# A second product accumulated in PSUM on a ScalarE copy of the first

## The chip, the cores and the metric

The kernel runs on one core of one Trainium2 chip. The metric is the device time of one execution in microseconds (us). The engines are called PE (TensorE), DVE (VectorE), ACT (ScalarE), POOL (GpSimd) and SP (SyncE); POOL and SP issue the transfers here. PSUM, the memory that PE writes, has eight banks of 128 x 512 float32.

## What is computed

One layer of a hybrid decoder on 512 tokens of 1024 channels, in float32, with 256 memory tokens beside them:

```python
h = rmsnorm(x);  proj = h @ w_in
y_a = (B * conv3(C * v)) @ w_a_out                 # short gated convolution
y_b = silu(layernorm(conv31(u * sigmoid(ug)) + bias)) @ w_b_out
y_c = attention(q, rmsnorm(mem) @ w_kv) @ w_att_out
x = x + (g0 * y_a + g1 * y_b + g2 * y_c) @ w_o     # g = sigmoid(gates of h)
gt, up = split(conv3(rmsnorm(x) @ w_up))
x = x + (silu(gt) * up) @ w_down;  return rmsnorm(x)
```

## The kernel before

**Precision.** Each operand of a product is split into a rounded high part and the rest. ACT makes the high part (`whi`, by a job `wh`, L621), DVE subtracts to get the low part (`wlo`, job `wl`, L625). Three matmuls (high x high, high x low, low x high) replace one.

**Quads.** The projections `w_in` and `w_up` are computed in 29 quads: 4 of `glu`, 4 of `cv`, 2 of `q`, 2 of `bb`, 6 of `gate` (the mixer) and 11 of `up` (the feed-forward part). A quad takes two column blocks of 256 and both halves of the tokens and of the 1024 inputs. In place of eight block products it makes seven, by a scheme of Strassen's kind: products of sums of weight blocks with sums of activation blocks, numbered 1, 2, 5, 6, 7, 4, 3. A product is 24 matmuls of 256 columns (`multiply`, L801).

The seven products go to three banks of PSUM. Bank `a` takes 1, then 6, 7 and 4 on top of it; bank `b` takes 5, then 3; bank `c` takes 2 alone. After a product the partial sum is read out (`quad_reads`, L820 to L853) into two SBUF tiles, `first` and `second`:

- `r1` (ACT, L828) copies bank `a` after product 1 to the first half of `first`.
- `r2` (DVE, L836) adds bank `c`, which holds product 2, to that half.
- `r5` and `r4` (ACT, L832, L851) copy to the halves of `second` with a minus; `r6` (ACT, L844) copies bank `a` after product 6 to the second half of `first`; `r7` and `r3` (DVE, L836) subtract and add.

Product 6 waits for `r1`, 7 for `r6`, 4 for `r7`, 3 for `r5`, since they write to the bank that was read. Neighbouring quads overlap on PE: the order is 6, 5 of the next quad, 7, 1 of the next, 4, 2 of the next, 3.

**The rest.** Before the quads stand keys and values from the memory tokens; between them the attention; a convolution of 31 taps in the mixer shared by ACT (products, `tp`, L1369) and DVE (sums, L1376); merge products (L1548 to L1550); the product with `w_o` (L572 to L574) in a seven-product scheme of its own; RMSNorm and transposes; the up quads with their three-tap convolution (L1498, L1504), `silu` and the gated tile `z` (L1867); and the product with `w_down` (L572 to L574, operands `zh` and `zl`, L2054 and L2061).

**Weights.** SP loads blocks of 512 KB (`ld`, L651), and POOL adds other blocks on top of them in flight by accumulating DMAs (L759), so that sums of weight blocks cost no engine time. A POOL DMA waits until the block's earlier use has been split.

**Order.** Each piece of work is a job with an engine, a cost and the jobs it waits for (`Jobs`, L226). PE's sequence is written out by hand (`seq`). A planner (`run`, L324) issues the others in the order of planned start, with ties by a due time: the latest start that PE's sequence allows, shifted by an entry of the table `LATER` for each kind of job (L73); `AHEAD` (L154) bounds for some kinds how early they may come. Buffers are rings of places (`take`), among them `ps`, the eight banks. The order so found on each engine is fixed in the program.

Of the kernel before, what the change touches and what calls it, by code (L numbers as in the profile page):

```python
# [67 lines left out]
UNIT_BUFS = 4  # L68
SUMS_BY_VECTOR = [("glu", 0)]
# [4 lines left out]
    "ACT c3": 3.05, "ACT cf": 151.64, "ACT csq": -59.81, "ACT exp": -90.93, "ACT fh h b00": 71.92,  # L74
    "ACT fh h b10": 0.49, "ACT fh h b11": -0.54, "ACT fh h t5": 18.75, "ACT fh h t6": -5.1,
    "ACT fh h2 t4": -0.3, "ACT fh h2 t5": -104.69, "ACT fh h2 t6": -37.81, "ACT fh h2 t7": -75.17,
    "ACT high": -1310.89, "ACT kh": -15.95, "ACT m root": -362.05, "ACT mgh a": -219.21,
    "ACT mgh b": -0.99, "ACT mgh c": 21.87, "ACT mgh d": -153.36, "ACT mgh e": 33.21,
    "ACT mgh f": -62.81, "ACT mgh g": -271.76, "ACT mh": 3.42, "ACT msq": 232.67,
    "ACT mu high": 145.56, "ACT oh": -157.89, "ACT pth": -125.46, "ACT qh": -99.6,  # L80
# [7 lines left out]
    "ACT sg": -62.24, "ACT sigmoid": -52.69, "ACT silu": 7.01, "ACT sq": -24.79, "ACT sr": -61.22,  # L88
    "ACT swish": -187.08, "ACT tap 0": 386.19, "ACT tap 1": -305.81, "ACT tap 3": -118.04,
# [9 lines left out]
    "ACT xroot": -139.83, "ACT xsq": -336.93, "ACT xsquare": -212.34, "ACT zh a": -65.22,  # L99
    "ACT zh b": -2.97, "ACT zh c": -129.55, "ACT zh d": -36.36, "ACT zh f": 1.48,  # L100
    "ACT zh g": -16.33, "DVE CV": -940.31, "DVE c3": -2.4, "DVE centre": 2.27, "DVE cf": -142.45,
# [5 lines left out]
    "DVE hd": -408.91, "DVE kl": -59.89, "DVE kt": 2.68, "DVE low": -1070.51,  # L107
    "DVE m scale": 21.29, "DVE mgl a": -99.36, "DVE mgl b": -1.83, "DVE mgl c": 45.17,
    "DVE mgl e": 12.48, "DVE mgl f": 89.83, "DVE mgl g": -183.96, "DVE ml": -76.45,
    "DVE ms c": 2.23, "DVE ms d": -43.26, "DVE ms e": -77.92, "DVE ms f": -596.02,  # L110
    "DVE msum": 32.2, "DVE mu fold": 229.47, "DVE mu low": 174.53, "DVE mu sum": 0.09,
    "DVE ol": -67, "DVE pn": -423.21, "DVE ptl": -21.53, "DVE ql": -21.16, "DVE r2 bb": -162.25,
# [6 lines left out]
    "DVE rl": -49.63, "DVE s6 glu": 1.12, "DVE sum": -306.61, "DVE sv": 1.24, "DVE tap 2": -81.17,  # L119
    "DVE tap 3": -12.91, "DVE top": -207.51, "DVE tot1": 70.89, "DVE tot2": -61.79,  # L120
    "DVE um": 13.54, "DVE v scale": -106.89, "DVE var fold": -2.02, "DVE var sum": 76.06,
# [8 lines left out]
    "DVE wsum": 473.99, "DVE x scale": -1037.6, "DVE x1 a": -18.75, "DVE x1 b": 243.92,  # L130
    "DVE x1 c": -180.74, "DVE x1 d": -17.54, "DVE x1 e": -112.02, "DVE x1 f": 46.27,
    "DVE x1 g": 20.12, "DVE xn": 3.93, "DVE xnorm": -39.32, "DVE xsum": -37.83,
    "DVE ymul": -36.44, "DVE ys": -4.73, "DVE z": -64.04, "DVE zd": -330.65, "DVE zl a": -650.04,
    "DVE zl b": -204.45, "DVE zl c": -3.74, "DVE zl d": -392.26, "DVE zl e": -2.42,
    "DVE zl f": -3.2, "DVE zl g": 10.21, "DVE zs d": -29.57, "DVE zs e": 108.61,
    "NONE c3": -206.17, "NONE cf": -314.68, "NONE mem tile": -186.16, "NONE raw tile K": -214.01,
    "NONE raw tile V": -229.8, "NONE rows": -24.01, "NONE sums": 290.26, "NONE temps": 154.52,
# [6 lines left out]
    "POOL wadd x": 0.53, "POOL wadd y": -89.15, "POOL wl merge 0": -554.82,  # L144
# [7 lines left out]
}  # L152

AHEAD = {  # L154
# [2214 lines left out]
```

## Time and profile before

| | us |
|---|---|
| median of 3 runs | 898.55 |
| lowest and highest | 898.41, 900.51 |
| the profiled execution | 899.25 |
| its span in the profile | 897.5 |

The span is what lies between the first and the last instruction of the profile; the other 1.75 us of that execution lie around it. The granted clock of PE was 0.999 of full speed. In the profile's groups, a line such as "L801 PE MATMUL bank<-ft6h,whi" names the line of the code, the engine, the operation and the tiles written and read, then the count, the busy time and the mean of one. In the chain of waits and the timeline the first number is the start, the second the duration.

### The profile page before, as it was taken

To read this page: it belongs to the slowest core of one execution; us is meant where nothing else is said; L and a number is where in the kernel's file an instruction comes from. 1 tells how busy PE (TensorE), PEld (TensorE's weight loads), DVE (VectorE), ACT (ScalarE), POOL (GpSimd) and SP (SyncE) were. 2 spreads that over 40 slices of the span, in tenths; PEclk is the share of its full clock that TensorE was granted. 3 is DMA by queue.
4 is the path that set the end of the run, shared out by engine and by line. 5 is a ranking of instruction groups with operands and counts; after the bars stand their busy time and mean duration, and the time that the engine had idled before them with its cause. 6 is when DMAs were issued, how large, how long until landed. Compare 5 with 4: busy or idle time off the path is not lost.

```text
span 897.5 us, 16787 instructions
## 1 busy us (share of the span) xinstructions
PE 888.1 (99%) x6677; PEld 849.2 (95%) x6677; DVE 835.6 (93%) x953; ACT 666.2 (74%) x911; POOL 126.7 (14%) x153
## 2 busy tenths in 40 slices
PE   8999999999999999999999999999999999999997
PEld 8999999999989999999899988899999999998886
DVE  6897999999999999999997888998899889999998
ACT  7677988989997888767856933777676676766566
POOL 0011121111011211111100001021221121002310
PEclk9999999999999999999999999999999999999999
DMA  9979698866688887988966498399999986769982
GB/s 356 379 184 261 137 224 193 214 157 116 164 203 242 198 177 168 211 218 208 230 127 183 141 338 206 102 234 286 307 241 250 221 174 125 197 243 333 257 196 94
DMA packets 54366, 190.60 MB, mean 212 GB/s; under 512 B 6160, under 2 KB 6544, under 8 KB 54288
## 3 DMA queue, kind: packets, MB, share of 16 engines
q0 software_dynamic: 20880, 75.24, 46.3%
q1 hardware_dynamic: 33120, 114.02, 35.2%
q8 instruction: 52, 0.85, 0.4%
q10 hardware_dynamic: 288, 0.27, 0.1%
q14 instruction: 26, 0.21, 0.1%
HBM read 185.31 MB, written 4.19 MB: 211 GB/s over the span
## 4 chain that ended last, share of the span: by engine, by line
PE 90%; DMA 5%; issue 2%; ACT 1%; DVE 1%; POOL 0%; SPq 0%; DVEq 0%; POOLq 0%; ACTq 0%
PE bank L801 56%; PE bank L572 6%; PE bank L574 6%; PE bank L573 6%; PE bank L1548 5%; PE bank L1550 5%; PE bank L1549 5%; PE bank L1059 2%; DMA wo<-in_w_o 2%; DMA ('up', 3)_946_7137<-in_w_up 1%; DMA wf<-in_w_up 1%; DMA mem<-in_mem_t 1%; PE ss L930 0%; ACT whi L621 0%; DVE wlo L625 0%
## 5 line engine op out<-in xcount | busy, mean ns | idle before, releaser
L621 ACT CAST whi<-wf 128x1024 fp32r<-128x1024 f32 x204 | 211.7, 1044 | 75.7 <-PE bank L801 30.7
L625 DVE TENSOR_TENSOR wlo<-wf,whi 128x1024 fp32r<-128x1024 f32 x198 | 239.1, 1215 | 16.2 <-ACT whi L621 16.1
L1369 ACT ACTIVATE tp<-u,pk 128x507 f32<-128x507 f32 (+22 forms) x184 | 119.8, 708 | 6.6 <-DVE acc L1376 5.3
L1376 DVE TENSOR_TENSOR acc<-acc,tp 128x1022 f32<-128x1022 f32 (+21 forms) x92 | 109.3, 1192 | 1.7 <-ACT tp L1369 0.4
L759 POOL DMA_DIRECT2D wf<-in_w_in x54 | 47.4, 903 | 234.6 <-DVE wlo L625 159.2
L801 PE MATMUL bank<-ft6h,whi 128*128 128x256 f32 x232 | 63.9, 275 | 0.2 <-ACT gt L828 0.2
L801 PE MATMUL bank<-ft5h,wlo 128*128 128x256 f32 x232 | 63.9, 275 | 0.2 <-DVE wlo L625 0.2
L801 PE MATMUL bank<-fb10h,whi 128*128 128x256 f32 x232 | 64.0, 276 | 0.0
L801 PE MATMUL bank<-fb11h,whi 128*128 128x256 f32 x232 | 64.0, 276 | 0.0
L801 PE MATMUL bank<-ft5l,whi 128*128 128x256 f32 x232 | 63.9, 275 | 0.0
L801 PE MATMUL bank<-fb00h,whi 128*128 128x256 f32 x232 | 63.9, 275 | 0.0
L801 PE MATMUL bank<-ft6h,wlo 128*128 128x256 f32 x232 | 63.8, 275 | 0.0
L801 PE MATMUL bank<-fb00l,whi 128*128 128x256 f32 x232 | 63.8, 275 | 0.0
L801 PE MATMUL bank<-fb00h,wlo 128*128 128x256 f32 x232 | 63.8, 275 | 0.0
L801 PE MATMUL bank<-fb10l,whi 128*128 128x256 f32 x232 | 63.8, 275 | 0.0
L801 PE MATMUL bank<-fb10h,wlo 128*128 128x256 f32 x232 | 63.8, 275 | 0.0
L801 PE MATMUL bank<-ft6l,whi 128*128 128x256 f32 x232 | 63.8, 275 | 0.0
L801 PE MATMUL bank<-ft7l,whi 128*128 128x256 f32 x232 | 63.8, 275 | 0.0
L801 PE MATMUL bank<-ft7h,wlo 128*128 128x256 f32 x232 | 63.8, 275 | 0.0
L801 PE MATMUL bank<-fb11l,whi 128*128 128x256 f32 x232 | 63.8, 275 | 0.0
L801 PE MATMUL bank<-fb11h,wlo 128*128 128x256 f32 x232 | 63.8, 275 | 0.0
L801 PE MATMUL bank<-ft7h,whi 128*128 128x256 f32 x232 | 63.8, 275 | 0.0
(378 smaller groups left out, 3134.8 us busy)
## 6 DMA issues: line engine op xcount, KB each, us to landing
wf<-in_w_in SPq DMA_DIRECT2D x58, 512.0 KB, 5.0
wf<-in_w_in POOLq DMA_DIRECT2D x54, 512.0 KB, 6.7
wf<-in_w_up SPq DMA_DIRECT2D x29, 512.0 KB, 8.3
wf<-in_w_up POOLq DMA_DIRECT2D x28, 512.0 KB, 7.5
wf<-in_w_down SPq DMA_DIRECT2D x15, 512.0 KB, 4.7
wf<-in_w_att_out SPq DMA_DIRECT2D x8, 512.0 KB, 3.6
wf<-in_w_a_out SPq DMA_DIRECT2D x8, 512.0 KB, 4.2
wf<-in_w_b_out SPq DMA_DIRECT2D x8, 512.0 KB, 4.6
```

The costliest lines, as they stand in the source:

```text
L572: nc.tensor.matmul(ps, s_hi, w_hi, start=start, stop=False, skip_group_check=again)
L573: nc.tensor.matmul(ps, s_hi, w_lo, start=False, stop=False, skip_group_check=again)
L574: nc.tensor.matmul(ps, s_lo, w_hi, start=False, stop=stop, skip_group_check=again)
L621: nc.scalar.copy(parts[0], src())
L625: nc.vector.tensor_tensor(lo, src(), hi.bitcast(F32), op=ALU.subtract)
L759: nc.gpsimd.dma_start(out=tiles[key], in_=block(w, col[c], k), accum_op=ALU.add)
L801: nc.tensor.matmul(ps[:, c, :], w[:, k, at], in_turns(a[k]), start=first and n == 0, stop=i == 3 and n == 2, skip_group_check=again,)
L1369: nc.scalar.activation(two(("tp", p, s))[:, j, s:], two(("u", p))[:, j, : SEQ - s], AF.Copy, scale=weight(j),)
L1376: nc.vector.tensor_tensor(a, a, two(("tp", p, s))[:, :, s:], op=ALU.add)
L1548: nc.tensor.matmul(ps, w_hi[:, i, at], hi, start=first, stop=False)
L1549: nc.tensor.matmul(ps, w_hi[:, i, at], lo, start=False, stop=False)
L1550: nc.tensor.matmul(ps, w_lo[:, i, at], hi, start=False, stop=last)
```

## The change

A list `SEEDED` names 25 of the 29 quads: all but `glu` 0 and `up` 0 to 2. In these, `r1` no longer reads bank `a` into SBUF: ACT copies it to bank `c` (`seed`). Product 2 does not start bank `c` anew, but accumulates on the copy, and waits for it. `r2` becomes a copy by ACT from bank `c` to the first half of `first`; DVE's addition is gone. `r6` comes after `r2`. Bank `c` is taken by `r1` instead of by product 2, and only a bank that has been written whole before may be taken for it. The quads' numbers of products, matmuls and transfers stay. The tables `LATER` and `AHEAD` are replaced as a whole (314 entries became 305, 183 became 189), and so the order on ACT, DVE, POOL and SP changes through much of the kernel; PE's does not.

```diff
+SEEDED = (
+    [("glu", p) for p in range(1, 4)] + [("cv", p) for p in range(4)]
+    + [(s, i) for s in ("q", "bb") for i in range(2)]
+    + [("gate", br, i) for br in range(3) for i in range(2)] + [("up", q) for q in range(3, 11)]
+)
...
     def multiply(q, f, act):
-        if f in (1, 2, 5):
+        if f in (1, 5) or f == 2 and not seeded(q):
             make(("bank", q, BANK_OF[f]))
...
-                first = f in (1, 2, 5) and i == 0 and c == 0
-                again = not (f in (1, 2, 5) and c == 0)
+                starts = f in (1, 5) or f == 2 and not seeded(q)
+                first = starts and i == 0 and c == 0
+                again = not (starts and c == 0)
...
+        new = f in (1, 5) or f == 2 and not seeded(q)
+        if f == 2 and not new:
+            after.append(("r1", q))
...
+        def seed():
+            make(bank("c"))
+            nc.scalar.copy(tiles[bank("c")], tiles[bank("a")])
+
+        def read2():
+            make(first)
+            nc.scalar.copy(parted(f()[:, :, lo_t]), turned(view("c")))
...
-        job(("r1", q), "ACT", actv(512), read1, [(q, 1)] + list(after),
-            take=[(first, ring)], use=[bank("a")])
-        job(("r2", q), "DVE", dve(512), lambda: add(f()[:, :, lo_t], view("c")),
-            [(q, 2), ("r1", q)], use=[bank("c"), first])
+        if seeded(q):
+            job(("r1", q), "ACT", actv(512), seed, [(q, 1)],
+                take=[(bank("c"), "ps=whole")], use=[bank("a")])
+            job(("r2", q), "ACT", actv(512), read2, [(q, 2)] + list(after), take=[(first, ring)],
+                use=[bank("c")])
+        else:
...
-            [(q, 6), ("r1", q)], use=[bank("a"), first])
+            [(q, 6), ("r2" if seeded(q) else "r1", q)], use=[bank("a"), first])
```

More of the change, by code (lines that the diff above doesn't have):

```diff
@@ L130 @@
[L130 to L135, printed above, removed]
@@ L136 @@
-    "NONE c3": -206.17, "NONE cf": -314.68, "NONE mem tile": -186.16, "NONE raw tile K": -214.01,
-    "NONE raw tile V": -229.8, "NONE rows": -24.01, "NONE sums": 290.26, "NONE temps": 154.52,
[6 rows of a table removed]
-    "POOL wadd x": 0.53, "POOL wadd y": -89.15, "POOL wl merge 0": -554.82,
[7 rows of a table removed]
+    "ACT c3": -120.1, "ACT cf": -509.48, "ACT csq": -53.11, "ACT exp": -0.12,
[3 rows of a table added]
+    "ACT high": -129.98, "ACT kh": 44.12, "ACT m root": -65.33, "ACT mgh a": 248.53,
+    "ACT mgh c": -45.79, "ACT mgh d": -1.43, "ACT mgh e": -192.03, "ACT mgh f": 103.98,
@@ new lines @@
+    "ACT zh d": -45.26, "ACT zh e": -187.1, "ACT zh f": 0.48, "ACT zh g": 68.1, "DVE CV": -69.32,
+    "DVE c3": -40.82, "DVE centre": 122.92, "DVE cf": -0.49, "DVE csum": 200.17,
[4 rows of a table added]
+    "DVE h2 t7": -15.33, "DVE hd": 32.93, "DVE kl": -10.05, "DVE kt": 5.38, "DVE low": -7.04,
+    "DVE m scale": -20.41, "DVE mgl a": -153.33, "DVE mgl b": 81.29, "DVE mgl c": -1,
+    "DVE mgl d": -391.03, "DVE mgl e": -106.25, "DVE mgl f": -46.38, "DVE mgl g": -1.35,
+    "DVE ml": -0.46, "DVE ms c": -5.01, "DVE ms d": 100.31, "DVE ms e": 16.38, "DVE ms f": 12.55,
@@ L152 @@
+    "DVE zs e": -0.21, "NONE cf": -18.86, "NONE mem tile": -38.05, "NONE raw tile V": 2.42,
+    "NONE rows": -0.56, "NONE sums": -330.92, "NONE temps": 8.24, "POOL ea": -45.14,
[5 rows of a table added]
+    "POOL s7 gate": 2.29, "POOL s7 glu": 77.65, "POOL s7 up": 14.62, "POOL wadd e": 41.57,
+    "POOL wadd x": -254.48, "POOL wadd y": 2.91, "POOL wl merge 0": 0.18,
[7 rows of a table added]
 }
 AHEAD = {
-    "ACT exp": 3.5, "ACT fh h b10": 3.6, "ACT fh h b11": 39.1, "ACT fh h t6": 101,
-    "ACT fh h t7": 3.8, "ACT fh h2 t6": 5, "ACT fh h2 t7": 5.3, "ACT high": 1.2, "ACT m root": 51,
@@ L179 @@
-    "DVE sv": 46.7, "DVE top": 52, "DVE tot2": 2.2, "DVE var fold": 1.2, "DVE weigh": 2.6,
[7 rows of a table removed]
-    "NONE c3": 37.8, "NONE cf": 145.6, "NONE raw tile K": 18.2, "NONE raw tile V": 49.2,
-    "NONE rows": 111.3, "POOL s3 glu": 1.2, "POOL s5 glu": 13, "POOL s5 q": 3.9,
[6 rows of a table removed]
+    "ACT cf": 1.6, "ACT csq": 21, "ACT exp": 3.2, "ACT fh h b00": 3.2, "ACT fh h b11": 118,
+    "ACT fh h t4": 1.9, "ACT fh h t6": 48.2, "ACT fh h t7": 7.3, "ACT fh h2 t6": 135.2,
+    "ACT fh h2 t7": 113.1, "ACT high": 61, "ACT m root": 1.3, "ACT mgh b": 19.4,
@@ new lines @@
+    "ACT mgh c": 26.6, "ACT mgh d": 1.1, "ACT mgh e": 10.6, "ACT mh": 16.4, "ACT msq": 1.3,
+    "ACT mu high": 39.9, "ACT pth": 13.7, "ACT qh": 4.2, "ACT r1 bb": 7.8, "ACT r1 cv": 58.5,
[3 rows of a table added]
+    "ACT r5 glu": 58.2, "ACT r5 q": 2.4, "ACT r6 bb": 78.9, "ACT r6 gate": 4, "ACT r6 glu": 31.6,
+    "ACT rh": 1.4, "ACT rm": 57, "ACT sa": 85.7, "ACT sr": 24.9, "ACT tap 2": 17.1,
[4 rows of a table added]
+    "ACT wh0 V": 80.4, "ACT xroot": 4.8, "ACT xsq": 73.9, "ACT zh a": 1.4, "ACT zh c": 101.7,
[3 rows of a table added]
+    "DVE h2 t7": 41.6, "DVE hd": 123.7, "DVE kl": 1.5, "DVE lns": 92.3, "DVE mgl e": 15.9,
@@ new lines @@
+    "DVE mgl f": 3.9, "DVE ml": 2, "DVE ms c": 21.9, "DVE ms f": 23.2, "DVE msum": 4.9,
+    "DVE mu fold": 1.7, "DVE mu low": 1.3, "DVE ol": 8.2, "DVE ptl": 150.2, "DVE ql": 1,
[3 rows of a table added]
+    "DVE var fold": 9.9, "DVE vl": 8.1, "DVE weigh": 6.3, "DVE wl V 0": 39.9,
[4 rows of a table added]
+    "DVE x1 g": 3.2, "DVE xnorm": 16.7, "DVE xsum": 2.8, "DVE ys": 15.9, "DVE z": 1.5,
+    "DVE zl c": 5.6, "DVE zl d": 2.8, "DVE zl e": 86.4, "DVE zl f": 76.9, "DVE zl g": 88.4,
+    "DVE zs d": 100.8, "DVE zs e": 3.6, "NONE c3": 147.6, "NONE cf": 1.5, "NONE raw tile K": 5.3,
@@ L195 @@
+    "NONE raw tile V": 16.1, "NONE rows": 1.1, "NONE sums": 2.6, "NONE temps": 2.6,
[3 rows of a table added]
+    "POOL wadd x": 58, "POOL wadd y": 19, "POOL wl merge 2": 10.7, "POOL xa": 15.7,
[4 rows of a table added]
 }
@@ L301, in latest_starts, with partly @@
         return due, users
+    def partly(self, name):
+        return name[0] in ("ss", "rows") or name[1] in ("warm", "end")
     def free_places(self, ring, leave=0):
+        ring, _, whole = ring.partition("=")
         own, _, other = ring.partition("+")
         own, other = (
-            [(at, r, i) for r in rs.split() for i, at in self.rings[r].items()]
+            [(at, r, i) for r in rs.split() for i, at in self.rings[r].items()
+             if not whole or i in self.written]
             for rs in (own, other)
@@ L393, in run @@
                 self.place[name] = ring, i
+                if ring == "ps":
+                    (self.written.discard if self.partly(name) else self.written.add)(i)
             code = self.tc.nc.cur_bb.bb.instructions
@@ L812, in multiply_job @@
             after.append(("fl", act, OPERAND[f]))
+        new = f in (1, 5) or f == 2 and not seeded(q)
+        if f == 2 and not new:
+            after.append(("r1", q))
         after += {6: [("r1", q)], 7: [("r6", q)], 4: [("r7", q)], 3: [("r5", q)]}.get(f, [])
         pe((q, f), 24 * MM_QUAD, lambda: multiply(q, f, act), after,
-           take=[(bank, "ps")] if f in (1, 2, 5) else [], use=[] if f in (1, 2, 5) else [bank],
-           unit=unit)
+           take=[(bank, "ps")] if new else [], use=[] if new else [bank], unit=unit)
     form_ready = {}
@@ L836, in add @@
             nc.vector.tensor_tensor(parted(t), parted(t), turned(b), op=op)
-        job(("r1", q), "ACT", actv(512), read1, [(q, 1)] + list(after),
-            take=[(first, ring)], use=[bank("a")])
-        job(("r2", q), "DVE", dve(512), lambda: add(f()[:, :, lo_t], view("c")),
-            [(q, 2), ("r1", q)], use=[bank("c"), first])
+        if seeded(q):
[4 more added lines that the diff above has]
+        else:
+            job(("r1", q), "ACT", actv(512), read1, [(q, 1)] + list(after),
+                take=[(first, ring)], use=[bank("a")])
+            job(("r2", q), "DVE", dve(512), lambda: add(f()[:, :, lo_t], view("c")),
+                [(q, 2), ("r1", q)], use=[bank("c"), first])
         job(("r5", q), "ACT", actv(512), read5, [(q, 5)] + list(after),
```

48 lines of the change are left out of this document (15 added, 33 removed), and 146 rows, old and new, of tables (AHEAD, LATER).

## The prediction

> **What bounds the kernel now.** I read the page's engine line first, then the table of what TensorE (PE) waited for, then counts of PE's instructions in chosen windows.
>
> ```profile
> span 897.5 us, 16787 instructions
> ...
> PE 888.1 (99%) x6677; PEld 849.2 (95%) x6677; DVE 835.6 (93%) x953; ACT 666.2 (74%) x911; POOL 126.7 (14%) x153
> ```
>
> PE is busy for 888.1 of 897.5 us, VectorE (DVE) for 93%, ScalarE (ACT) for 74%. Busy time of PE proves little, since a matmul's end is modelled (its row says 275 ns) while the next starts earlier. So I count starts.
>
> ```profile
> 62.00:162.00 100.00, 100.00 (x898) 1.00 0.89 205
> 320.00:420.00 100.00, 100.00 (x898) 1.00 0.86 200
> 606.00:656.00 50.00, 49.61 (x442) 1.00 1.05 288
> 632.00:782.00 150.00, 150.00 (x1343) 1.00 0.88 212
> 805.00:811.00 6.00, 5.43 (x24) 1.00 1.03 416
> ```
>
> These are windows with PE alone: stretch, length, busy time and count. In 150 us of pure quad work stand 1343 matmuls of 256 columns, one per 0.1117 us; two other stretches give the same rate. Nothing is lost there. Two places do lose: 606 to 656 has 442 where 50 / 0.1117 = 447.6 fit, so 5.6 x 0.1117 = 0.63 us; 805 to 811 has 24 of the 512-column kind, one per 0.216 us (0.22 in the chain below), where 27.8 fit, so 0.82 us.
>
> ```profile
> PE bank L574 <- DVE zl L2061: 0.4, 1, 0.4
> PE bank L801 <- ACT gt L828: 0.2, 1, 0.2
> PE bank L572 <- DVE x L1761: 0.2, 1, 0.2
> PE bank L572 <- ACT zh L2054: 0.2, 1, 0.2
> PE bank L801 <- DVE wlo L625: 0.2, 1, 0.2
> ```
>
> These are PE's waits (waited for, us in total, times, longest); the table agrees: behind the head only five waits are seen at all, one of them (0.2, at L1761) outside those two places. So the body holds 0.63 + 0.82 + 0.2 = 1.65 us of counted loss. A wait under 0.16 us (0.275 - 0.112) hides inside a matmul's modelled duration; with a dozen of those at changes of stage I estimate at most 4 us in all. That is the ceiling of any gain in a kernel whose PE work stays the same.
>
> The Trainium skill ("Trainium Kernel Development and Optimization", Performance Expectations) calls matmul busy time a bad metric and the share of the weight loads a good one. By it 897.5 - 849.2 = 48 us would be open. The counts above disagree: where PE starts a matmul every 0.1117 us without a miss there is no room, whatever the loads' row adds up to.
>
> The two losses have these causes, by the chain of waits:
>
> ```profile
> 616.32 13.06 DMA ('up', 3)_946_7137<-in_w_up
> ...
> 629.45 1.07 ACT whi L621
> ...
> 630.54 1.24 DVE wlo L625
> ```
> ```profile
> 805.50 0.23 PE bank L574
> ...
> 805.78 0.58 issue
> 806.35 1.22 DVE z L1867
> 807.57 0.94 DVE wlo L625
> ...
> 808.62 0.96 DVE zl L2061
> ```
>
> Near 620 to 632 a weight block for the first quads of the up-projection lands late. Near 806 DVE is late with the last gated tile `z`.
>
> **The change part by part.** The order of the built instructions has the same 349 PE jobs in the same sequence in both kernels, so no matmul goes and none is added. DVE has 25 fewer jobs (`r2`), ACT 25 more.
>
> ```profile
> L836 DVE TENSOR_TENSOR gt<-gt,bank 128x512 f32<-128x512 f32 x22 | 15.0, 682 | 1.8 <-PE bank L801 1.8
> L844 ACT COPY gt<-bank 128x512 f32<-128x512 f32 x11 | 6.4, 584 | 2.8 <-PE bank L801 2.1
> L828 ACT COPY gt<-bank 128x512 f32<-128x512 f32 x11 | 6.4, 592 | 5.0 <-PE bank L801 5.0
> L1212 ACT ACTIVATE pr<-bank,cols 128x256 f32<-128x256 f32 x16 | 7.4, 473 | 0.5 <-DVE cols L1206 0.5
> ```
>
> (1) Removed: 25 additions of 0.682 us, 17.1 us of DVE. All of it lies beside PE, so by itself it is worth 0, except where DVE ends a PE wait. That is the place at 806: eight of the seeded quads are up quads, 8 x 0.682 = 5.5 us that DVE no longer has between 632 and 800, and 0.82 us is lost there. I take all of it: -0.82. What is late next there is the weight split (`wlo`, 0.94 in the chain).
>
> (2) Added: for each quad a copy from bank to bank, and the old copy to SBUF moves behind product 2. A copy with a bank as destination does not occur in this trace. The nearest rows, bank to SBUF with the same 128x512, say 0.584 and 0.592; I take 0.59 for each, 25 x 0.59 = 14.8 us of ACT, 74% of the span becoming 76%. The ends: 0.47, what half the columns take from a bank (L1212), and 1.07, a 128x1024 copy (L621 in the chain above). Hidden under PE in either case as long as the new wait holds.
>
> (3) The new wait: product 2 now waits for the seed, the seed for product 1. In the sequence one product (4 of the quad before) stands between them, at two quads four more short jobs. Product 4's length, from the chain, and the timeline at a copy that already waits in this way:
>
> ```profile
> 53.88 2.68 PE bank L801 x24
> ```
> ```profile
> 101.67 0.28 PE L801 MATMUL bank<-ft6h,wlo 128*128 128x256 f32 x1
> ...
> 101.98 0.59 ACT L844 COPY ug<-bank 128x512 f32<-128x512 f32 x1 [0.86 <-PE bank L801]
> ```
>
> One product is 2.68 us. ACT starts 0.31 us after the start of product 6's last matmul, that is 0.2 after the next matmul could start. From 2.68 go these 0.2, the copy's 0.59 and some 0.1 back to PE, so the seed may start 1.8 us late before PE stands. A copy of 1.07 would leave 1.3. The same geometry exists already: product 7 waits for `r6` (L844), `r6` for product 6, with one product between. The trace names who waited for any of the 29 `r6`:
>
> ```profile
> who waited for it (us, times):
>   POOL wf L759: 5.8, 1
>   ACT whi L621: 0.7, 1
> ```
>
> PE is not among them. In the built order, at each of the 25 seeds at least one weight copy (`wh`, 1.07 us) stands on ACT between the seed and the start of product 2, so the seed is not the last thing ACT does before the deadline. Behind a late seed on ACT's queue stand that weight copy and its split on DVE, needed about two products later. I take 0 for the wait, with 25 x 0.3 = 7.5 us as the far end if ACT is late at every seed.
>
> (4) Bank `c` is held from the seed on, one product earlier (2.68 us), and until ACT, not DVE, has read it. Eight banks; a quad pair in flight uses five. No PE wait in the table is for a bank: 0, up to one copy (0.59 us) now and then.
>
> (5) Moved: both tables of due times are replaced, so on each engine much of the order changes: 502 of 719 ACT jobs, 566 of 856 DVE jobs, 121 of 145 POOL and 156 of 220 SP jobs keep their relative order. Bytes and DMA count stay. For the late place at 620 to 632 the built order puts `u` of up 3 nine products ahead of its use instead of four, and `v` of up 2 forty-one instead of ten, but `u` of up 2 nine instead of thirty-three. The loss of 0.63 can vanish or grow; I take -0.5, with +1.8 for each block that comes one load later:
>
> ```profile
> 600.00:650.00 50.00, 49.61 (x441) 49.23 (x441) 44.21 (x50) 34.00 (x45) 10.44 (x12) 1.00 1.05 291
> 200.00:250.00 50.00, 50.00 (x368) 47.60 (x368) 48.55 (x63) 47.83 (x81) 4.75 (x6) 1.00 0.63 150
> ```
>
> A 512 KB block at the 291 GB/s of that window is 1.8 us. For the wait of 0.2 at L1761 I take the loss away: -0.2.
>
> Sum: -0.82 + 0 + 0 + 0 - 0.5 - 0.2 = -1.5 us. The profiled execution took 899.25 us (897.5 of span, 1.75 around it), so it would become 897.7. The median of the runs shown is 898.55, 0.7 below the profiled one, so the forecast is **897.0 us**.
>
> **The rivals.** (a) *All stalls go.* The new order removes the whole 4 us: 894.5. For it: DVE, with 48.55 of 50 us from 200 to 250, is the engine that leaves the planner the least choice, and it is eased. Against: the losses at changes of stage are chains of dependent steps, not load.
>
> (b) *Weights late.* The forecast's +1.8 happens in the up-projection: SP and POOL take the blocks in another order, and DMA is already at a share of 1.05 from 600 to 650. Price 1.8 us for a block that comes one load later; it decides from the second block on. With three, 897.0 + 5.4 = 902.4: slower. For it: `u` of up 2 moved 24 products nearer to its use. Against: other blocks moved the other way, and the bytes are the same.
>
> (c) *Seeds late.* ACT, not DVE, becomes the bound where it is fullest: 47.83 of 50 us from 200 to 250 (row above). Three quads there add about 3 x 0.59 = 1.8, which makes 49.6 of 50. Once ACT is over 1.8 us behind at a seed, PE stands for the excess, and each later seed in the stretch with it. With 0.3 us at 25 seeds: 897.0 + 7.5 = 904.5. Against: most ACT work there are conv taps (`tp`), which can move to 250 to 300, where ACT has 9 us free:
>
> ```profile
> 250.00:300.00 50.00, 50.00 (x329) 46.54 (x328) 49.24 (x53) 40.62 (x60) 8.15 (x10) 1.00 0.84 213
> ```
>
> (d) *It does nothing for the time.* Stalls of the same size stand elsewhere: 898.5. This is inside the forecast's case.
>
> **How the numbers follow.** What a measurement here can tell from no change is about 0.3%, 2.7 us: below 895.85 is faster, above 901.25 slower. Forecast with (d): 0.52, its own range 895.9 to 901.2, since the gain must exceed 2.7 of an estimated 4 us to leave it below. (a): 0.25. (b): 0.14. (c): 0.09. So faster 0.25, same 0.52, slower 0.23. The low end is the ceiling of the gain, 894.5, less the scatter of the runs, so 894.0; the high end takes in (b) with three blocks, 902.5, and leaves out (c) and worse.
>
> **What would show it.** In the profile after: PE's count from 632 to 782 again near 1343, and no entry of PE for the bank-to-bank copy over 0.2 us in the table of waits (step 3). The bank-to-bank copy's row near 590 ns (step 2). No `zl` or `z` in PE's waits near 806 (step 1). ACT 14 us busier, DVE 17 us less. The forecast is wrong if PE's counts fall short in the 256-column stretches (seeds late), if a weight block's DMA stands in the chain between 580 and 640 for more than now (weights late), or if head or tail changed: PE's first product starts and the last output leaves about as far from the ends as before.

## The result, and the profile after

| | before | after |
|---|---|---|
| median, 22 executions each | 899.45 us | 901.06 us |
| lowest and highest | 898.24, 901.28 | 899.1, 905.18 |
| ratio (95% interval) | 1 | 1.0022 (1.0013 to 1.003) |
| the profiled execution, its span | 899.25, 897.5 | 901.15, 899.4 |

The changed kernel is slower by 0.22%. That is less than the 0.3% named above, but its interval leaves out 1, and the forecast of 897.0 lay on the other side. (The ratio is that of the means; the two medians alone give 1.0018.) Line numbers moved: the products of the quads are L819 (L801 before), `wh` L634, `wl` L638, the seed L852, the second read L856, VectorE's additions L864, `r6` L878.

Engine line and PE's waits of the changed kernel (waited for; us in total, times, longest):

```profile
span 899.4 us, 16769 instructions
...
PE 888.0 (99%) x6677; PEld 849.5 (94%) x6677; DVE 822.5 (91%) x928; ACT 678.3 (75%) x936; POOL 126.7 (14%) x153
```
```profile
PE bank L819 <- ACT bank L852: 1.2, 1, 1.2
PE bank L586 <- DVE wlo L638: 0.6, 1, 0.6
PE bank L819 <- ACT gt L848: 0.6, 1, 0.6
PE bank L587 <- DVE zl L2095: 0.4, 1, 0.4
...
PE bank L585 <- DVE x L1795: 0.2, 1, 0.2
```

DVE has 25 instructions fewer and is 13.1 us less busy, ACT 25 more and 12.1 us more busy. The first of these rows of waits is new: PE stood 1.2 us for a seed, once. The windows of the prediction, with PE alone, and the new place; behind them the new place in the kernel before:

```profile
320.00:420.00 100.00, 98.59 (x881) 1.00 0.84 199
400.00:406.00 6.00, 4.59 (x39) 1.00 0.76 186
606.00:656.00 50.00, 49.38 (x442) 1.00 1.05 283
632.00:782.00 150.00, 150.00 (x1345) 1.00 0.87 210
805.00:811.00 6.00, 5.66 (x25) 1.00 1.03 415
```
```profile
400.00:406.00 6.00, 6.00 (x56) 1.00 0.73 227
```

From 632 to 782 PE is as dense as before. From 320 to 420 it starts 881 matmuls, where before there were 898: 17 x 0.1117 = 1.9 us are gone, and they are gone between 400 and 406, where 39 stand and before 56 stood. The place at 606 to 656 still has 442, the place at 806 still its wait for `zl`. The chain of waits at 400 to 406:

```profile
393.23 8.42 DMA wf<-in_w_in
...
402.63 1.04 ACT whi L634
403.67 1.22 ACT tp L1403 x2
404.89 0.49 ACT bank L852
```

And ScalarE's own timeline (start, duration; in brackets the idle time before it and what ended it):

```profile
398.27 0.58 ACT L860 ACTIVATE g<-bank 128x512 f32<-128x512 f32 x1
401.67 2.00 ACT L634 CAST whi<-wf 128x1024 fp32r<-128x1024 f32 x2 [2.81 <-DMA wf<-in_w_in]
403.57 1.31 ACT L1403 ACTIVATE tp<-u,pk 128x499 f32<-128x499 f32 x2
404.79 0.57 ACT L852 COPY bank<-bank 128x512 f32<-128x512 f32 x1
```

A transfer lands at 401.65. ACT has stood 2.81 us for it with nothing to do. Then come two weight copies, two conv taps, and only then the seed of `gate (0,1)`. The seed could have used at most the last half microsecond of that idle time, since its product 1 ended only then. This is the last matmul of product 1:

```profile
400.82 0.28 PE L819 MATMUL bank<-fb00h,wlo 128*128 128x256 f32 x1
```

16 of the 25 seeds start 0.31 us after the start of such a matmul, so this one could have started at 401.1 (an estimate). It started at 404.79, because the 3.1 us of copies and taps ahead of it on the queue had not been done earlier. In the kernel before ACT stands for the same block as well, but no seed comes behind it:

```profile
400.02 2.95 ACT L621 CAST whi<-wf 128x1024 fp32r<-128x1024 f32 x3 [2.74 <-DMA wf<-in_w_in]
```

Product 1 starts at 398.41 there and at 398.25 here, so the first copy begins 1.6 us behind it before and 3.4 us after. The block itself was still in time for its own product: VectorE began to split it at 402.76, at some 1.2 us a split, and PE was free at 404.06. PE waited for the small copy behind it.

**Gaps.** To compare kernels I use one sum: for each two neighbouring matmuls the distance of their starts over the median of their kind (line and shape), as far as it is above 0.06 us. In us, by stretches, with the transfers' rate from 300 to 340 us:

| kernel | ratio to before | GB/s | 400-450 | 600-650 | 800-850 | all |
|---|---|---|---|---|---|---|
| before | 1 | 177 | 0 | 0.92 | 1.65 | 6.95 |
| after | 1.0022 | 146 | 2.25 | 0.88 | 1.36 | 8.01 |
| e1_no_wait | 1.0016 | 145 | 1.41 | 1.05 | 1.26 | 7.00 |
| e2_seed_ahead | 1.0021 | 146 | 1.69 | 2.62 | 1.24 | 9.05 |
| e3_no_additions | 0.9997 | 170 | 0 | 0.84 | 1.15 | 5.28 |
| e5_seeds_old_order | 1.0015 | 179 | 0.71 | 2.42 | 1.15 | 9.61 |
| e6_new_order_alone | 1.0098 | 142 | 2.47 | 2.10 | 1.47 | 15.14 |
| e7_old_loads | 1.0073 | 180 | 1.00 | 0.86 | 1.25 | 11.95 |
| e8_new_loads | 1.0010 | 165 | 0 | 2.18 | 1.65 | 7.46 |
| e9_old_loads_only | 1.0007 | 176 | 0.41 | 1.47 | 1.44 | 6.28 |
| e10_before_z_first | 1.0004 | 168 | 0.24 | 0.91 | 1.85 | 5.85 |
| e11_up_seeds | 0.9998 | 175 | 0.47 | 0.90 | 1.15 | 7.56 |
| e12_up_seeds_z_first | 1.0000 | 173 | 0 | 0.93 | 1.62 | 6.48 |
| e13_two_loads | 1.0024 | 159 | 2.31 | 2.57 | 1.24 | 9.27 |
| e14_two_loads_z | 1.0022 | 158 | 1.86 | 1.70 | 1.21 | 7.67 |

The gaps are those of one profiled execution, the ratios those of 4 to 12 executions each (22 for the changed kernel); 0.001 of ratio is 0.9 us. e4, whose order is broken throughout, has 39.3 in all and is left out of the table.

### The profile page after: what moved, and what is told of

It reads as the page before. It is cut to its first block, busy times and chain, and to the rows that moved or that the text cites. A ratio compares the mean times of both kernels' runs of the same rounds, so it can differ in the third digit from the quotient of the medians.

```text
span 899.4 us, 16769 instructions
## 1 busy us (share of the span) xinstructions
PE 888.0 (99%) x6677; PEld 849.5 (94%) x6677; DVE 822.5 (91%) x928; ACT 678.3 (75%) x936; POOL 126.7 (14%) x153
## 4 chain that ended last, share of the span: by engine, by line
PE 89%; DMA 5%; DVE 2%; issue 2%; ACT 1%; SPq 0%; DVEq 0%; ACTq 0%; POOLq 0%
PE bank L819 53%; PE bank L587 6%; PE bank L586 6%; PE bank L585 6%; PE bank L1582 5%; PE bank L1583 5%; PE bank L1584 5%; DMA wf<-in_w_up 2%; PE bank L1093 2%; DMA wf<-in_w_in 2%; DVE wlo L638 1%; DMA wf<-in_w_v 1%; ACT whi L634 1%; PE ss L964 0%; PE bank L1331 0%
## 5 line engine op out<-in xcount | busy, mean ns | idle before, releaser
L638 DVE TENSOR_TENSOR wlo<-wf,whi 128x1024 fp32r<-128x1024 f32 (+1 forms) x199 | 239.4, 1211 | 30.4 <-ACT whi L634 29.9
L634 ACT CAST whi<-wf 128x1024 fp32r<-128x1024 f32 (+1 forms) x205 | 212.3, 1043 | 71.3 <-PE bank L819 19.5
L1403 ACT ACTIVATE tp<-u,pk 128x482 f32<-128x482 f32 (+22 forms) x184 | 119.7, 707 | 5.3 <-DVE acc L1410 5.0
L1410 DVE TENSOR_TENSOR acc<-acc,tp 128x1022 f32<-128x1022 f32 (+22 forms) x92 | 109.2, 1187 | 1.6
L772 POOL DMA_DIRECT2D wf<-in_w_in x57 | 49.7, 888 | 280.5 <-DVE wlo L638 150.1
L819 PE MATMUL bank<-fb10h,whi 128*128 128x256 f32 x232 | 64.3, 277 | 1.2 <-ACT bank L852 1.2
L819 PE MATMUL bank<-ft6h,whi 128*128 128x256 f32 x232 | 63.9, 275 | 0.6 <-ACT gt L848 0.6
L819 PE MATMUL bank<-fb11h,whi 128*128 128x256 f32 x232 | 64.0, 276 | 0.0
L819 PE MATMUL bank<-fb00h,whi 128*128 128x256 f32 x232 | 63.9, 275 | 0.0
L819 PE MATMUL bank<-ft5h,wlo 128*128 128x256 f32 x232 | 63.8, 275 | 0.0
L819 PE MATMUL bank<-fb00l,whi 128*128 128x256 f32 x232 | 63.8, 275 | 0.0
L819 PE MATMUL bank<-fb10h,wlo 128*128 128x256 f32 x232 | 63.8, 275 | 0.0
L819 PE MATMUL bank<-fb10l,whi 128*128 128x256 f32 x232 | 63.8, 275 | 0.0
L819 PE MATMUL bank<-ft7h,whi 128*128 128x256 f32 x232 | 63.8, 275 | 0.0
L819 PE MATMUL bank<-fb11l,whi 128*128 128x256 f32 x232 | 63.8, 275 | 0.0
L819 PE MATMUL bank<-ft6l,whi 128*128 128x256 f32 x232 | 63.8, 275 | 0.0
L819 PE MATMUL bank<-ft5l,whi 128*128 128x256 f32 x232 | 63.8, 275 | 0.0
L819 PE MATMUL bank<-ft6h,wlo 128*128 128x256 f32 x232 | 63.8, 275 | 0.0
L819 PE MATMUL bank<-ft7h,wlo 128*128 128x256 f32 x232 | 63.8, 275 | 0.0
L819 PE MATMUL bank<-fb00h,wlo 128*128 128x256 f32 x232 | 63.8, 275 | 0.0
L819 PE MATMUL bank<-ft7l,whi 128*128 128x256 f32 x232 | 63.8, 275 | 0.0
L819 PE MATMUL bank<-fb11h,wlo 128*128 128x256 f32 x232 | 63.8, 275 | 0.0
```

Source lines behind the costliest of these rows:

```text
L634: nc.scalar.copy(parts[0], src())
L638: nc.vector.tensor_tensor(lo, src(), hi.bitcast(F32), op=ALU.subtract)
L772: nc.gpsimd.dma_start(out=tiles[key], in_=block(w, col[c], k), accum_op=ALU.add)
L819: nc.tensor.matmul(ps[:, c, :], w[:, k, at], in_turns(a[k]), start=first and n == 0, stop=i == 3 and n == 2, skip_group_check=again,)
L1403: nc.scalar.activation(two(("tp", p, s))[:, j, s:], two(("u", p))[:, j, : SEQ - s], AF.Copy, scale=weight(j),)
L1410: nc.vector.tensor_tensor(a, a, two(("tp", p, s))[:, :, s:], op=ALU.add)
```

## The experiments

The first theory, L: a late weight block holds ScalarE's queue, and product 2's new wait for the seed behind it turns that into standing time of PE. Its rivals: O, the new order costs, seeds or not; D, VectorE's relief was worth what step 1 said and was given away elsewhere. From e5 on the theories are W (the order of the weight loads) and S (the seeds themselves).

**e1_no_wait** and **e2_seed_ahead** attack the wait.

```diff
-            make(bank("c"))
-            nc.scalar.copy(tiles[bank("c")], tiles[bank("a")])
+            nc.scalar.copy(tiles[bank("a")], tiles[bank("a")])
```

> The changed kernel in its own order, but the 25 seeds copy bank a onto itself (same engine, size and place in the queue) and product 2 starts bank c fresh, so it waits for no seed; product 1's part in the first half is left out. Theory L (the wait: a late weight block holds ScalarE's queue and the seed in it, and PE stands because product 2 waits for the seed): no PE wait on a seed's line, the 1.35 us at 404 gone, about 0.4 left between 400 and 410, time 1.2 to 1.5 us below the changed kernel's. Theory O (the new order on the engines costs the time, with or without the wait): within 0.5 us of the changed kernel. If the seeds' wait costs more in other executions than in the profiled one, it is more than 1.5 us below.

e2 changes ScalarE's queue alone:

```diff
+MOVED = [(("r1", ("gate", 0, 1)), ("wh", (("gate", 0, 0), 3))),
+         (("wh", (("gate", 0, 1), 2)), ("wh", (("gate", 0, 0), 3))),
+         (("r1", ("gate", 1, 0)), ("tp", 3, 19))]
```

(A pair names a job and the job ahead of which it comes.)

> The changed kernel with three moves on ScalarE's queue: the seed of gate (0,1) comes ahead of the two weight copies and the two conv taps that stand between product 1 and it, and the seed of gate (1,0) ahead of two conv taps. Nothing else is changed. Theory L: PE's 1.35 us at 404 gone, PE's waits on the seed's line at most 0.2 us in all, time about 1.3 us below the changed kernel's. Theory O: the time is lost elsewhere, less than 0.5 us is won. Against L stands also that the weight copy, now behind the seed, comes up to 0.57 us later; it had 1.44 us to spare, so I expect no new wait for it.

Measured: e1 1.0016 (1.0007 to 1.0024), e2 1.0021 (1.0012 to 1.003): neither is parted from the changed kernel. In both no PE wait on the seed is left and the 1.35 us at 404 are gone, as L wanted. But the time comes back 10 to 16 us later, as O had it. In e1 PE stood 0.59 us at 414 and 0.42 at 420; the rows of its waits (L832 are the quads' products, L890 is `r6`, L876 VectorE's additions):

```profile
PE bank L832 <- ACT g L890: 0.4, 1, 0.4
...
PE bank L832 <- DVE g L876: 0.3, 1, 0.3
```

L is half right. The seed is where the lateness comes out first; without it `r6` and `r7` are late, by 0.84 us less in all (1.41 in place of 2.25). ACT and DVE are behind in this stretch, and the wait on the seed did not make them so.

**e3_no_additions** is the relief of VectorE by itself: the order of the kernel before without the 25 additions.

```diff
+LEFT_OUT = [("r2", q) for q in SEEDED]
...
+            if key in LEFT_OUT:
+                continue
```

> The kernel before in its own order, without the 25 additions on VectorE that the change takes away (product 2 is left out of the first half of those sums). This is the relief of VectorE alone. Theory D (the relief by itself is worth what the forecast's step 1 said): at least 0.8 us below the kernel before, and PE's gap at 806 gone. Theory L (PE is dense and the gap at 806 is a chain of dependent steps set by the order): 0 to 0.5 us below, the gap at 806 within 0.3 us of what it was (0.95 by starts); VectorE 17 us less busy.

Measured: 0.9997 (0.9987 to 1.0007). The gaps from 800 to 850 fell from 1.65 to 1.15, those at 806 alone from 0.95 to 0.56, and DVE's busy time from 835.6 to 824.0 us. The chain at that place:

```profile
804.77 0.08 issue
804.85 1.22 DVE z L1880
806.07 0.93 DVE wlo L638
807.01 0.12 issue
807.12 0.97 DVE zl L2074
```

Before, 0.58 us of "issue" stood ahead of `z`, now 0.08: that half microsecond was VectorE's load. The rest is a chain of dependent steps, which this relief did not shorten. D is refuted by the gap at 806, which should have gone. The time alone would not refute it: 17 us less on VectorE are worth 0.3 us, within -0.6 and 1.2, and D asked for 0.8.

**e4_seeds_old_tables** takes the changed code with the tables of the kernel before.

```diff
-    "ACT r1 up": 9.2, "ACT r2 bb": -86.56, "ACT r2 cv": -229.33, "ACT r2 gate": 148.27,
-    "ACT r2 up": 0.39, "ACT r4 bb": 34.02, "ACT r4 gate": 16.82, "ACT r4 glu": -1.12,
...
+    "ACT r1 bb": -215.84, "ACT r1 cv": -594.74, "ACT r1 gate": 433.52, "ACT r1 glu": 1.98,
+    "ACT r1 q": 90.43, "ACT r1 up": -207.53, "ACT r4 bb": 15.58, "ACT r4 cv": -145.25,
```

> The changed kernel's code with the two tables of due times of the kernel before, so the planner lays the seeds into the old order. Theory L (what counts is how far ahead of product 2 the seeds stand on ScalarE's queue): several PE waits on the seed's line, more than the changed kernel's 1.2 us in all, and a time at or above the changed kernel's, 901 to 906. Theory O (the new tables lose the time, the seeds cost nothing): the time of the kernel before, within 0.7 us.

Measured: 931.07 us, 1.0363 (1.0347 to 1.0379), far outside both expectations.

```profile
PE bank L820 <- ACT g L879: 14.1, 1, 14.1
PE bank L587 <- DVE wlo L639: 3.5, 4, 1.1
PE bank L820 <- ACT bank L853: 2.5, 2, 1.6
```

PE stood 14.1 us for one `r6` (L879) at 422, 2.5 us for two seeds (L853), and in many other places. The old tables shift `r1` for its old duty and have no entry at all for a second read on ACT. So this run does not price the seeds; it shows that the tables belong to the change.

**e5_seeds_old_order** and **e6_new_order_alone** part seeds and order. From here on the order is written out in a list, and jobs are moved in it by hand (in e10 behind the planner). In e5 each seed stands behind the start of the product after product 1, each second read where VectorE's addition stood:

```diff
 (("cv", 1), 1), (("cv", 0), 4),
+("r1", ("cv", 1)),
 (("cv", 1), 2), ("r4", ("cv", 0)), (("cv", 0), 3),
+("r2", ("cv", 1)),
```

> The order of the kernel before on every engine, written out, with only the 25 seeds laid into it: each seed on ScalarE right behind the start of the product after product 1, each second read on ScalarE where VectorE's addition stood. No other job moves and no table decides. Theory W (the changed kernel loses its time by the order of its weight loads: between 300 and 340 us the transfers move 146 GB/s where before they moved 177, and the blocks used at 390 to 425 come late): the time of the kernel before, within 0.6 us, and PE's waits on the seed's line at most 0.3 us in all. Theory S (the seeds themselves cost, through a wait that is on PE's path more often): at least 1 us above the kernel before, with PE waits on the seed's line.

```diff
-SEEDED = (
-    [("glu", p) for p in range(1, 4)] + [("cv", p) for p in range(4)]
...
+SEEDED = [("gate", 2, 0), ("gate", 1, 0), ("gate", 1, 1)]
```

> The order of the changed kernel on every engine, written out, without 22 of the 25 seeds: these quads read bank a into SBUF and add bank c on VectorE as before (three quads of the gates keep their seed, since without it the places in SBUF run out; VectorE has 15 us more to do). Theory W: the changed kernel's loss stays, 900.5 to 902, with 0.8 us or more of PE's gaps between 400 and 425. Theory S: the time of the kernel before, 899.2, within 0.6 us.

Measured: e5 1.0015 (1.0007 to 1.0023), between the two forecasts: some 1.4 us above the kernel before, where W allowed 0.6, and not by the wait that S named. There is no PE wait on a seed, but two new ones on the attention's softmax (`pr`, L1290). The chain of waits of e5 shows why:

```profile
167.59 1.02 ACT pr L1290 x4
168.60 0.55 ACT bank L896
169.15 0.97 ACT whi L678
...
172.79 1.94 ACT pr L1290 x8
174.73 0.04 issue
174.78 1.09 PE bank L1375 x8
```

A seed (L896) of 0.55 us stands in the softmax's chain, another of 0.48 us in the chain of the second place, and PE's gaps at 173 and 206 are 1.03 and 0.68 us. So ScalarE is not free of charge in the attention, though the prediction's window from 200 to 250 did not show it. e6: 1.0098 (1.0085 to 1.0111), gaps all through the kernel, the longest PE waits on VectorE's additions (L904):

```profile
PE bank L859 <- DVE g L904: 1.4, 2, 1.2
...
PE bank L859 <- DVE uu L904: 0.7, 1, 0.7
```

The new order supposes the relief: with the additions put back, VectorE is late in it. Neither W nor S had that; this run says nothing about the loss at 404, which in it has a different end (`r7` on VectorE, 1.2 us).

**e7_old_loads, e8_new_loads, e9_old_loads_only** exchange the order of the loads between 270 and 395 us. The part of SP's queue that differs, as quads and blocks:

```diff
 bb 0 s, cv 1 v,
-cv 1 r, bb 0 u, bb 0 v, cv 2 v, cv 3 v, cv 2 s, bb 0 r, cv 2 u, cv 2 r, cv 3 s, cv 3 u, bb 1 s,
+bb 0 u, cv 2 s, cv 1 r, bb 0 v, cv 2 u, cv 3 s, bb 0 r, cv 3 u, bb 1 s, cv 2 v, cv 2 r, cv 3 v,
 bb 1 u, gate 0 0 s
```

The line with a minus is the changed kernel's (and e8's), the one with a plus that of e7 and e9 (and of the kernel before). POOL's accumulating transfers are exchanged with them, and so is what the list keeps with each transfer: the finished job that it has to wait for, and its place in the rings. The runs do not part the order from these waits; "the order of the loads" below means both.

> The changed kernel in its own order, but the weight loads and accumulating transfers between PE's jobs 109 and 157 (about 270 to 395 us) in the order of the kernel before. Theory W: the transfers of 300 to 340 back to 170 GB/s or more, PE's gaps between 400 and 425 under 0.5 us (2.25 in the changed kernel), and a time 1 to 1.8 us below the changed kernel's ratio of 1.0022, so 1.0002 to 1.0011 of the kernel before. Theory S: no more than 0.4 us below it.

> The kernel before, without seeds and in its own order, but the weight loads and accumulating transfers between PE's jobs 109 and 157 in the order of the changed kernel. Theory W: 0.8 to 1.8 us above the kernel before, with PE's gaps between 400 and 425 that it did not have. Theory S: the time of the kernel before within 0.4 us.

> The changed kernel in its own order, but only the weight loads on SP and the accumulating transfers on POOL between PE's jobs 112 and 157 in the order of the kernel before; POOL's weight splits, which the earlier run of this kind had moved too (PE then stood 4.0 us at 256 for one of them), stay. Theory W (order of the loads): 175 GB/s or more from 300 to 340, PE's gaps between 400 and 425 at most 1.0 us, ratio to the kernel before 1.0004 to 1.0013 (the changed kernel has 1.0022). If the loss is ScalarE's load and not the blocks' arrival: gaps of 2 us stay at 400 to 425, ratio 1.0018 or more.

Measured: e7 1.0073 (1.0058 to 1.0089). The rate is 180 GB/s, the gap at 404 is gone, the gaps from 400 to 450 are 1.00. But the exchange had also put POOL's split of a merge block behind accumulations, and PE stood 4.0 us for it at 256. So e9, without that: 1.0007 (0.9996 to 1.0018). Rate, and PE's counts from 400 to 425 (busy times of PE, PEld, DVE, ACT, POOL with their counts, clock, DMA share, GB/s), first the changed kernel, then e9:

```profile
300.00:340.00 40.00, 40.00 (x361) 40.00 (x360) 39.46 (x42) 37.29 (x54) 6.45 (x8) 1.00 0.66 146
400.00:425.00 25.00, 23.59 (x206) 23.05 (x206) 23.20 (x25) 21.35 (x30) 1.73 (x2) 1.00 0.72 187
```
```profile
300.00:340.00 40.00, 40.00 (x360) 40.00 (x360) 39.46 (x43) 37.68 (x55) 6.08 (x7) 1.00 0.77 176
400.00:425.00 25.00, 25.00 (x223) 24.82 (x222) 24.51 (x25) 23.02 (x33) 1.73 (x2) 1.00 0.75 190
```

With 176 GB/s in place of 146, PE starts 223 matmuls instead of 206. ACT and DVE do the same jobs in the same order as in the changed kernel in this stretch; they only do them earlier. e9's seed of `gate (0,1)`:

```profile
399.20 2.02 ACT L678 CAST whi<-wf 128x1024 fp32r<-128x1024 f32 x2 [2.14 <-DMA wf<-in_w_in]
401.12 1.32 ACT L1447 ACTIVATE tp<-u,pk 128x499 f32<-128x499 f32 x2
402.35 0.57 ACT L896 COPY bank<-bank 128x512 f32<-128x512 f32 x1
```

It still stands behind the weight copies and taps, but comes 2.4 us sooner. e8, the other way round, has a rate between the two (165 GB/s) and loses nothing at 400: 227 matmuls stood from 400 to 425 before, and 226 here. In e8 the block is not late at all:

```profile
398.88 3.08 ACT L665 CAST whi<-wf 128x1024 fp32r<-128x1024 f32 x3 [1.57 <-DMA wf<-in_w_in]
```

Measured from the start of product 1 of `gate (0,1)`, ACT begins the first copy of this block after 1.6 us in the kernel before, 3.4 in the changed one, 2.2 in e7, 1.6 in e9 and 0.8 in e8. So the loss at 404 needs both, the new order of the loads and the new order on ACT and DVE, and only together do they make the block late. Whether the old order on ACT and DVE would have absorbed a late block no run shows. e8's ratio is 1.0010 (1.0002 to 1.0019). The place where its profile loses more than that of the kernel before is at 622 to 624, 1.64 us in place of 0.40; that the ratio comes from there is not shown, since this loss comes and goes (last section). The intervals of e9 and of the changed kernel overlap by 0.0005; what parts them is the gaps, in e7 and e9 alike, and 0.44 us at the end of the program (last section), which is no part of the loss at 404.

**e13_two_loads** asked whether one block is to blame that the changed kernel loads 24 jobs ahead of its use.

```diff
-cv 2 v, cv 3 v, cv 2 s, bb 0 r, cv 2 u, cv 2 r, cv 3 s, cv 3 u, bb 1 s, bb 1 u
+cv 2 v, cv 2 s, bb 0 r, cv 2 u, cv 2 r, bb 1 s, cv 3 s, cv 3 u, cv 3 v, bb 1 u
```

> The changed kernel with two of SP's loads moved and nothing else: the block v of cv 3 comes 18 of PE's jobs later (it was loaded 24 jobs ahead of its use and held one of the six places all that time), and the block s of bb 1 takes the freed place 11 jobs earlier. Theory W, in its narrow form (one block loaded far too early starves the queue from 300 to 340): 165 GB/s or more from 300 to 340 (146 in the changed kernel), PE's gaps at 400 to 425 at most 1.0 us (2.25), ratio 1.0005 to 1.0014. If the loss needs the whole order of the loads: gaps of 1.5 us or more stay there and the ratio is 1.0016 or more.

Measured: 1.0024 (1.0015 to 1.0032), 159 GB/s, gaps of 2.31. The narrow form of W is refuted: these two loads are not enough. Which of them would do, short of all, is open.

**e10_before_z_first, e11_up_seeds, e12_up_seeds_z_first, e14_two_loads_z** are about step 1, the place at 806.

```diff
-wl b 3, z 10, wl a 4, zl a 2
+z 10, wl a 4, zl a 2, wl b 3
```

> The kernel before with one job moved on VectorE: the split of the weight block b 3 of the last product comes behind the last gated tile's low part instead of ahead of the gated tile z. VectorE's work is the same. If order sets the gap at 806 (theory L): the two gaps there (0.35 and 0.60 us by starts) fall to 0.5 or less together, ratio 0.9988 to 0.9996. If VectorE's load sets it (theory D, the forecast's step 1): unchanged, ratio within 0.0004 of 1.

```diff
+SEEDED = [("up", q) for q in range(3, 11)]
```

> The order of the kernel before on every engine, with only the eight seeds of the up-projection laid into it; all other quads as before. This is the forecast's step 1 with its real price: 5.5 us less for VectorE and 4.7 us more for ScalarE between 632 and 800, no seed in the attention's stretch. Forecast's step 1: the gaps at 806 (0.95) gone, ratio 0.9991. Theory W with the bare relief as measured: gaps at 806 about 0.56, no gap on a seed's line, ratio 0.9993 to 1.0000. Theory S: ScalarE late, new gaps at the reads after product 6 between 640 and 800, ratio over 1.0005.

> The run before with the one move on VectorE besides (the split of the weight block b 3 behind the last gated tile's low part). If relief and order take different parts of the gap: ratio 0.9985 to 0.9992, nothing over 0.3 us left at 806. If they take the same part: the ratio of the move alone.

e14 is e13 with the order `z 10, wl a 4, zl a 2, wl b 3` (the changed kernel has `wl a 4, z 10, wl b 3, zl a 2`).

> The run before with VectorE's order at the last product changed besides: the last gated tile z ahead of the split of block a 4, the split of b 3 behind z's low part. If order alone sets the gap at 808 (1.05 us by starts in the changed kernel): under 0.5 us there and 0.0006 below the run before. If VectorE is full there, as the same kind of move in the old order suggests (the gap came back 4 us later): as much loss between 805 and 820 as before, ratio within 0.0004 of the run before.

Measured: e10 1.0004 (0.9995 to 1.0012). The two gaps at 806 are gone, and a gap of 1.28 us stands at 812.6, where the moved split is now late:

```profile
PE bank L586 <- DVE wlo L638: 1.1, 1, 1.1
```

e12, 1.0000 (0.9992 to 1.0009), has the same 1.28 us at 813.1. In e14, 1.0022 (1.0013 to 1.0032), the gaps that e13 has at 811 and 812 come back as 0.15 at 820 and 0.60 at 839.8; the stretch loses 1.21 in place of 1.24. VectorE's timeline in e10 has no idle time from 805.6 to 814:

```profile
805.63 1.22 DVE L638 TENSOR_TENSOR wlo<-wf,whi 128x1024 fp32r<-128x1024 f32 x1
806.77 0.95 DVE L2074 TENSOR_TENSOR zl<-z,zh 128x768 fp32r<-128x768 f32 x1
807.64 1.22 DVE L638 TENSOR_TENSOR wlo<-wf,whi 128x1024 fp32r<-128x1024 f32 x1
808.77 0.95 DVE L2047 TENSOR_TENSOR z<-z 128x768 f32<-128x768 f32 x1
...
812.78 1.29 DVE L638 TENSOR_TENSOR wlo<-wf,whi 128x512 fp32r<-128x512 f32 x2
```

Each row begins before the one ahead of it has ended, by 0.08 us in the first two. What one job gains there another loses: order alone does not set this gap, and relief in the 168 us before it took away half a microsecond in e11, while with z first, in e12, the stretch from 800 to 850 loses 1.62 in place of 1.65. e11, 0.9998 (0.9989 to 1.0006), keeps what e3 showed: 1.15 in place of 1.65, no wait on a seed. In its profiled execution, 900.41 us where the median is 898.4, PE stood 1.81 us for `r6` at 395, in a stretch where the order is that of the kernel before. VectorE was late there already: at 389 ACT had stood 2.34 us for a result of it, where the kernel before has 0.96 us, and a conv tap that waits for VectorE stands ahead of `r6` on ACT's queue. Why VectorE was late in that execution is open. No version here is measurably faster than the kernel before; e11 and e12, with eight seeds, are faster than the changed one beyond both intervals, e9 by its median.

## Why the prediction was wrong

The ceiling held: all gaps together moved between 5.3 and 9.6 us except where an order was broken (e4, e6, e7). The sign failed in the steps that were set to a gain or to nothing.

- **Step 1 (-0.82 at 806)** was the first failure: the two gaps at 806 hold 1.05 us where they held 0.95, and the stretch from 800 to 850 loses 1.36 in place of 1.65. The prediction took the whole loss for VectorE's load and named the weight split as next, without asking whether it would be late. The runs show 0.5 us of load over the whole stretch (e3, e11); the rest is a chain at a place where VectorE is full (e10, e14).
- **Step 2 (0.59 us a copy)** was right: 570 ns in the trace, and the copy's only wait is the one of step 3. VectorE's busy time fell by 13.1 us (11.6 in e3), not 17.1: neighbouring rows of VectorE overlap by some 0.08 us (e10's rows above), so that a row taken away leaves less than its length. As an estimate, 25 times 0.682 less an overlap at either end is 13.0.

```profile
L852 ACT COPY bank<-bank x25: 570/570/602, 72.5 to 773.4; 128x512 f32<-128x512 f32 x25
```

- **Step 3 (0 for the new wait)** failed at one seed of 25, by 1.35 us; a second, at 424, was only just in time. The prediction saw that a weight copy always stands near the seed, and asked what is queued behind a late seed. It did not ask what is queued *ahead* of it and waits for something slower: a transfer. "1.8 us late before PE stands" was right as a number (17 of 25 seeds had 1.9 us left or more), but this seed came 3.7 us later than it could have, by the estimate above. The existing waits of this geometry, for `r6`, were taken for proof that there is room; e1 shows PE standing for `r6` as well, 0.4 us, when ACT is late, and so does e11's profile.
- **Step 4 (0)** was right: no row of PE's waits names the copy that now frees bank `c` (L856).
- **Step 5 (-0.5)** was the step that failed by most. The place it looked at, 606 to 656, kept its 442 matmuls. The loss came 200 us earlier, at 400 to 425, where the kernel before had none: 2.25 us, of which step 3's 1.35 are a part. The prediction compared orders of loads near places that were already late and took the rest of the order for harmless. e9 shows the cause in the order of the loads from 270 to 395, with the waits that go with it: with the old loads the gaps from 400 to 450 fall from 2.25 to 0.41. e8 shows that it takes the new order on ACT and DVE besides. The wait at L1761 (-0.2) stayed, now as L1795.
- Of the rivals, (a) did not come: PE's gaps grew from 6.95 to 8.01. (b) named the right thing, a weight block that comes too late, at the wrong place and with the seed as the one who pays; (c)'s stretch, 200 to 250, lost nothing, though in e5, where no table makes room for the seeds, PE stands 1.7 us in the attention with a seed in the chain both times.

The sum by gaps: -0.36 in the first 50 us, -0.14 from 150 to 250, +2.25, -0.20 from 550 to 650, -0.18 behind it, -0.29 from 800 to 850, and +0.44 behind PE's last matmul (below): 1.5 of the 1.9 us by which the two spans differ. The rest lies in gaps under 0.06 us, nearly all of it in the first 50 us. PE's 6677 matmuls come in the same sequence in both kernels, so their starts can also be compared one by one: the changed kernel is 0.02 us ahead after 50 us, 2.09 behind at 425, 1.42 behind at PE's last matmul, and 1.86 at the end.

## What to carry to other kernels

Where PE starts its matmuls without a miss, work taken from another engine is worth only what that engine ends on PE's path, here 0.5 of 17 us by PE's gaps; look first whether the place that is late is full or only a chain. A new wait on a short copy is as late as what stands ahead of the copy on its engine's queue: read what the instructions ahead of it wait for, transfers above all, and not only how long they take. And an order made for one load of the engines is part of the change: with the old tables the same seeds cost 32 us, without the seeds the new order costs 9.

## What the runs showed of the hardware

- **The last instruction block.** From the start of PE's last matmul to the end of the span 5.97 to 5.98 us pass in the kernel before and in e3, e4, e5 and e7 to e12, but 6.41 to 6.42 in the changed kernel and in e1, e2, e6, e13 and e14, with the same work on all engines. In all sixteen the last packet of the output starts 4.67 or 4.68 us after that matmul, so the 0.44 us lie behind the output. In the last 2.5 us of the changed kernel one packet of an instruction queue stands behind the output:

```profile
q1 hardware_dynamic: 144, 0.13, 15.7%
q10 hardware_dynamic: 42, 0.05, 6.1%
q14 instruction: 1, 0.01, 1.2%
```

Such a packet is recorded at the end of all six of those kernels, in e2 and e6 just behind the span, and of none of the other ten. The Trainium skill ("Runtime: NRT & Kernel Launch", Instruction fetch mechanics) says that a sequencer fetches its program in blocks by its own DMA queue, at a cost that is mostly hidden. Here 0.44 us would not be hidden. But the packet starts at the earliest 0.02 us before the end of the span, when the 0.44 us are all but over. It marks the six kernels; that it is the cause is not shown, and no run moved it.

- **Loss that comes and goes.** From 600 to 650 the gaps are 0.84 to 1.05 us in eight of the profiled executions of the table and 1.47 to 2.62 in seven; which it is does not follow the kernel's order there (e8's is that of the kernel before). In the seven PE waits there for `r1` of an up quad, 0.5 to 1.2 us, and in six of them for a weight split right behind, 0.4 to 0.5 us. What decides it stays open, and it is as large as the whole effect of the change.

- **A copy from bank to bank** took 570 ns at the median in the changed kernel (25 seeds, 570 to 602). The 25 copies from a bank to SBUF at L856 took 560 to 607 ns there. The Trainium skill ("ScalarE: Activation LUTs", Step-by-step: what each stage is for) calls ScalarE's way to PSUM the faster one; the rows here do not part the two, since the ranges overlap and the second kind reads the bank in another order of its columns.
